# A hybrid encoder layer: the gate product placed eight expert blocks earlier, and its empty tiles lent to the expert loads

## The chip, the cores and the metric

The kernel runs on one core of one Trainium2 chip. The metric is device time in microseconds of that core, the median of several runs of one program. The engines are called as in the profile: PE (TensorE, matrix products), PEld (its weight loads), DVE (VectorE), ACT (ScalarE), POOL (GpSimd) and SP (SyncE, which here only issues transfers).

## The reference

One encoder layer on 512 tokens of width 1024. Attention comes first and is not touched. What matters is the part behind it:

```
q = xb @ w_q                                   # keys of 8 heads
v1, i1 = top_k(q1 @ sub_keys[0].T, 16)         # 16 of 128 first halves
v2, i2 = top_k(q2 @ sub_keys[1].T, 16)         # 16 of 128 second halves
cv, ci = top_k(v1[:, None] + v2[None, :], 16)  # 16 of 256 pairs -> expert e1*128 + e2
g   = softmax(cv)
act = g * gelu(xb . u_table[idx])
ffn = sum(act * v_table[idx])                  # 16384 experts, 128 per token
gate = sigmoid(h @ ple_gate_w + ple_gate_b)
h = layer_norm(alpha * h + ffn + gate * (p @ ple_w))
```

## The kernel before

The 512 tokens are four chunks of 128. Chunk 0 gets its expert rows by gathers from memory. For the other three chunks the whole expert table is multiplied: U block `i` (128 experts, 512 KB) times the tokens gives 128 x 256 values for chunks 2 and 3, and GELU of them is kept or written to memory (`ge_dram`). A matrix G (token by expert, the softmax weights) is built from products of one-hot tiles (`oh`, `ow_hi`, `ow_lo`) and written to memory (`g_dram`). Chunk 1 takes its first-layer values by gathered rows (128 of them, index tile `s_ix`), which land in six tiles (`whi`, `wlo`, `row`, two of each).

The change lies in the middle stage, from 414 to 909 us, which does all of this at once. Its order is written by hand in a manual schedule, in which every engine runs what it is given in the order of the program:

- DVE's own order is: routing of chunk 2 (`route`, the top-16 searches), building G of chunk 2 (`build_g`, 16 steps, each with a one-hot tile, two weighted tiles and a group of 16 products on PE), routing of chunk 3, building G of chunk 3, routing of chunk 0, building G of chunk 1. Row gathers of POOL and their dot products on DVE (L970) are put between these steps.
- PE gets, between these steps, `run_pe(amount)` worth of other work from one generator, `gate_and_leads`: 104 U blocks (`lead_block`, L1042, eight products over the tile `whole`), and the gate product in 16 sections of 12 products each (`mm<-g_hi,...`, L124 to L126). A section takes one weight tile (`g_raw`, 256 KB, L1063), cut by ACT into `g_hi` (L1070) and by DVE into `g_lo` (L1071). There is one `g_hi` and one `g_lo`, and three `g_raw`. Two U blocks stand behind each section (`STRIDE = 2`), and a third behind the eighth and the sixteenth, the two *gate ends*, where four 256 KB tiles `pl` are loaded (`gate_end`, L1079) and added by DVE with the bias tile `gb`.
- The first `FIRST` U blocks stand ahead of the gate. Fifteen blocks of the table were loaded long before into tiles that were empty then (`early`, `ge_ring`, `g_hi`, `base`); the order of blocks takes two of these and one fresh one in turn, until they are used up.
- SP issues the loads. A fresh U block goes to one of three tiles `raw` (`load_u`, L1015); `lead_block` issues loads until three are held, so that SP waits at each for PE to finish the block three before.
- Behind the gate, `own_h` splits `whole` again into the tiles `hTh`, with a copy on ACT (L1109) and a subtraction on POOL (L1113), in two halves, as tasks put between the blocks: the first half six blocks behind the gate's last task, the second two blocks later. POOL's row gathers stand before, between and behind them in its queue.

The tasks are taken one at a time, at every second product of a U block:

```
while sum(x[1] for x in held_u.values()) < 3 and to_load:
    load_u()
...
    if k % 2 and tasks:
        tasks.pop(0)()
    yield PRODUCT_U
```

Of the kernel before, what the change touches and what calls it, by code (L numbers as in the profile page):

```python
# [9 lines left out]
F32 = mybir.dt.float32  # L10
# [26 lines left out]
WIDE = 40  # L37
LEAD = 104
SPILL = 72
FIRST = 30  # L40
STRIDE = 2
PACE = 1.07
AHEAD = 14.0
# [35 lines left out]
def tile_encoder_layer(ctx: ExitStack, tc: tile.TileContext, A: dict, out: bass.AP):  # L79
    nc = tc.nc  # L80
# [104 lines left out]
    def ps_tile(name, bufs=2):  # L185
        return ps6.tile([128, 512], F32, name=name, bufs=bufs)
# [88 lines left out]
    with tc.tile_pool(name="ln0", bufs=1, reuse_waits="tile") as ln0:  # L275
# [5 lines left out]
        for c in range(4):  # L281
            layer_norm(h[c], eg, eb)
            transpose_to(hTh, hTl, h[c], c)
            if c == 0:
                for kk in range(4):
                    raw = wst.tile([128, 2, 512], F32, name="raw", bufs=3)
# [315 lines left out]
    for kk in range(4):  # L602
        w = stream(A["w_o"][kk * 256:(kk + 1) * 256, 0:512].rearrange("(k p) n -> p k n", p=128), [2, 512])
        for k2 in range(2):
            k = 2 * kk + k2
# [94 lines left out]
    rw = pR.enter_context(tc.tile_pool(name="rw", bufs=1, reuse_waits="tile"))  # L700
    h_s = rw.tile([128, D], F32, name="h_s")
    gb = rw.tile([128, D], F32, name="gb")
# [137 lines left out]
    for g in range(16):  # L840
# [7 lines left out]
        raw = wst.tile([128, 8, 128], F32, name="raw", bufs=3)  # L848
# [150 lines left out]
    gating = True  # L999
    held_u = {}  # L1000
# [7 lines left out]
    to_load = [i for i in lead_ids if i >= EARLY]  # L1008
    first_load = to_load[0]

    def load_u(name="raw"):
        if to_load:
            i = to_load.pop(0)
            raw_t = wst.tile([128, 8, 128], F32, name=name, bufs=3 if name == "raw" else 2)
            ins = nc.sync.dma_start(raw_t, A["uT"][i])  # L1015
            if i == first_load:
                tc.keep_in_program_order(ins)
            held_u[i] = ([raw_t[:, k] for k in range(8)], name == "raw")

    def leave_u(i, ps):  # L1020
        if i % 2 == 0:
            ge_t[i] = (ge_kept if SPILL <= i < KEPT else ge_free).pop(0)
        nc.scalar.activation(ge_t[i - i % 2][:, i % 2], ps[:, :N_U], AF.Gelu)  # L1023
        if i < SPILL and i % 2:
            x = ge_t.pop(i - 1)
            nc.scalar.dma_start(ge_dram[i // 2], x.rearrange("p b t -> p (b t)"))
            ge_free.append(x)
# [3 lines left out]
    def lead_block():  # L1031


        while sum(x[1] for x in held_u.values()) < 3 and to_load:
            load_u()
        if not lead_ids:
            return
        i = lead_ids.pop(0)
        raw = early_u[i] if i < EARLY else held_u.pop(i)[0]
        ps = psH.tile([128, 512], F32, name="hp") if gating else ps_tile("mm", 4)  # L1040
        for k in range(8):
            nc.tensor.matmul(ps[:, :N_U], raw[k], whole[:, k, :], start=(k == 0), stop=(k == 7))  # L1042
            if k == 3 and last:
                leave_u(*last.pop())
# [3 lines that stand above are left out]
        last.append((i, ps))  # L1048
# [11 lines left out]
    def gate_raw(j):  # L1060
        raw = rw.tile([128, 512], F32, name="g_raw", bufs=3)
        k = j % 8
        nc.sync.dma_start(raw, A["gate_w"][k * 128:(k + 1) * 128, j // 8 * 512:(j // 8 + 1) * 512])  # L1063
        return raw

    def gate_cut(raw):

        hi = rw.tile([128, 512], F32R, name="g_hi")
        lo = rw.tile([128, 512], F32R, name="g_lo")
        return (hi, lo), [lambda: nc.scalar.copy(hi, raw),  # L1070
                          on_vector(0.6, lambda: nc.vector.tensor_tensor(lo, raw, r32(hi), op=OP.subtract))]  # L1071
# [49 lines left out]
    def gate_and_leads():  # L1121
        nonlocal gating
        graw = [gate_raw(0), gate_raw(1)]
        for n in range(FIRST):
            if n == FIRST - 2:
                w, cut = gate_cut(graw.pop(0))
                tasks.extend([cut[0], nothing, cut[1]])
            yield from lead_block()
        for j in range(16):
            if j % 8 == 0:  # L1130
                while tasks:
                    tasks.pop(0)()
                gps = [ps_tile("mm", 4) for _ in range(4)]
            k = j % 8
            for c in range(4):
                cs = slice(c * 128, (c + 1) * 128)
                mm3(gps[c], (hTh[:, k, cs], hTl[:, k, cs]), w, k == 0, k == 7)
                yield PRODUCT_G
            if j + 1 < 16:
                w, cut = gate_cut(graw.pop(0))  # L1140
                if j + 2 < 16:
                    graw.append(gate_raw(j + 2))
                tasks[0:0] = [cut[0], nothing, cut[1]]
            if k == 7:
                gate_end(gps, slice(j // 8 * 512, j // 8 * 512 + 512))
                yield from lead_block()
            for _ in range(STRIDE):
                yield from lead_block()
# [32 lines left out]
    with tc.manual_schedule(engines={nc.vector.engine, nc.scalar.engine, nc.tensor.engine, nc.sync.engine,  # L1181
                                     nc.gpsimd.engine}):
        for _ in range(3):
            load_u()
# [63 lines left out]
    def load_v(n):  # L1248
        raw = wst.tile([128, D], F32, name="raw", bufs=3) if in_wst(n) else pV.tile([128, D], F32, name="v_raw", bufs=3)
        nc.sync.dma_start(raw, v_rows[order[n] * 128:(order[n] + 1) * 128, :])  # L1250
        return raw
# [55 lines left out]
    with tc.manual_schedule(engines={nc.vector.engine, nc.scalar.engine, nc.tensor.engine, nc.sync.engine,  # L1307
                                     nc.gpsimd.engine}):
        gating = True
        for name in ("whi", "whi", "wlo", "wlo"):  # L1310
            load_u(name)
        some = [fetch_u(0, BESIDE + k) for k in range(SOME)]
        for lo, hi in ((128 // GT, NTG), (0, 128 // GT)):
            load_g(0, lo, hi, nc.gpsimd)
        blocks_ahead(2)
        v_next = [load_v(n) for n in range(2)]
        for u in range(SOME):
            gather_u(0, BESIDE + u, some[u])
        blocks_ahead(2)
        v_next.append(load_v(2))  # L1320
        v_cut = {}
        for n in range(2):
            v_cut[n] = cut_v(n)
            blocks_ahead(1)
        for k in range(BESIDE + SOME, PRE):
            gather_u(0, k)
        for _ in pe_work:
            pass
# [7 lines left out]
    with tc.manual_schedule(engines={nc.vector.engine, nc.sync.engine}):  # L1336
# [3 lines left out]
        for n, i in enumerate(order):  # L1340
            if g_tiles and n == g_tiles[0][0]:
                n0, _, views, j = g_tiles.pop(0)
                gt = views[j]
            raw = v_next[n] if n < 3 else load_v(n)
# [149 lines left out]
```

## Time and profile before

| what | value |
|---|---|
| median of 3 runs | 1522.99 us (1522.4 to 1523.95) |
| profiled execution, its own time | 1525.05 us |
| its span, first to last instruction | 1523.2 us |
| mean granted TensorE clock | 0.990 |
| PE / DVE / ACT / POOL busy | 95% / 83% / 36% / 41% |
| bytes moved by DMA | 456 MB, mean 299 GB/s |

A row of a timeline reads: start in us, duration in us, engine, line, operation, the tile written and the tiles read, how many in a row; in brackets the idle time before it and who ended it. Matmuls are pipelined: their durations overlap, so that the pace of PE is read from the starts of successive rows. A line of windows gives a stretch, then the busy time of each engine with its count of instructions, the mean granted TensorE clock, the busy share of the DMA engines and the GB/s. One product of an fp32 U block stands in the trace as two PE instructions, so a U block is 16 of them. In the middle stage 414:507 is the routing of chunk 2, 507:591 building its G, 591:660 and 660:755 the same for chunk 3, 755:796 the routing of chunk 0, 796:878 building G of chunk 1, 878:909 the blocks left over.

### The profile page before, as it was taken

How to read it: one execution, taken by the hardware profiler on the slowest of the kernel's cores; microseconds unless marked ns; L12 is line 12 of the kernel's file. 1: busy time of each engine (PE TensorE's matmuls, PEld its weight loads, DVE VectorE, ACT ScalarE, POOL GpSimd, SP SyncE). 2: the span in 40 equal slices, each digit the busy share in tenths (PEclk: the TensorE clock that was granted, in tenths of full speed). 3: DMA queues.
4: the chain of work that ended last, by engine and by line, in shares of the span. 5: the costliest groups of instructions: out<-in, count | busy, mean ns of one | idle time of the engine just before them, and what ended most of it. 6: DMA issues, size and time to landing. Idle time of an engine off the chain costs nothing.

```text
span 1523.2 us, 21811 instructions
## 1 busy us (share of the span) xinstructions
PE 1451.8 (95%) x7715; PEld 1221.4 (80%) x7715; DVE 1267.5 (83%) x2638; ACT 544.4 (36%) x893; POOL 627.7 (41%) x537
## 2 busy tenths in 40 slices
PE   6999999999999999898989989999999999999996
PEld 4788777788888888687877868898788888888875
DVE  7376795668999999899779938988789999989998
ACT  3265685333311232222322323444333333333333
POOL 1013110043355644253235345655545555556560
PEclk9999999999999999899999999999999999999999
DMA  7233241194389999899879999999999999999992
GB/s 238 66 115 92 86 125 43 49 300 147 105 291 322 394 416 413 301 396 398 314 258 409 412 388 392 391 392 335 341 389 396 402 398 398 402 396 400 394 362 113
DMA packets 188414, 456.15 MB, mean 299 GB/s; under 512 B 16400, under 2 KB 80272, under 8 KB 185232
## 3 DMA queue, kind: packets, MB, share of 16 engines
q1 hardware_dynamic: 121264, 211.45, 38.8%
q0 software_dynamic: 58400, 208.69, 36.3%
q10 hardware_dynamic: 8640, 34.61, 5.6%
q8 instruction: 61, 1.00, 0.3%
q14 instruction: 49, 0.40, 0.1%
HBM read 413.01 MB, written 38.80 MB: 297 GB/s over the span
## 4 chain that ended last, share of the span: by engine, by line
PE 42%; DVE 20%; issue 15%; DMA 14%; POOL 6%; ACT 2%; SPq 1%; POOLq 0%; DVEq 0%; ACTq 0%
DMA raw<-in_v_rows_dram 7%; PE acc L126 5%; PE acc L124 5%; PE acc L125 5%; PE pj L124 3%; PE pj L125 3%; PE pj L126 3%; DMA raw<-in_uT_dram 3%; DVE base L1277 3%; PE mm L1042 3%; POOL row L968 2%; PE mm L124 2%; PE mm L126 2%; POOL wlo L968 2%; PE mm L125 2%
## 5 line engine op out<-in xcount | busy, mean ns | idle before, releaser
L1275 POOL DMA_INDIRECT gat<-in_v_rows_dram,i_sel x128 | 192.8, 1506 | 140.8 <-DVE base L1277 119.5
L1042 PE MATMUL hp<-whole,raw 128*128 128x256 f32 x816 | 193.4, 393 | 21.1 <-DMA raw<-in_uT_dram 21.1
L1260 POOL DMA_INDIRECT gat<-in_u_rows_dram,i_sel x97 | 149.4, 1541 | 121.8 <-DVE gat L1266 93.6
L1042 PEld LDWEIGHTS hp<-whole,raw 128*128 128x128 f32 x816 | 158.9, 197 | 45.6 <-issue 13.2
L126 PE MATMUL acc<-v_hi,a_lo 128*128 128x512 f32 x456 | 178.4, 392 | 2.6 <-DVE a_lo L110 2.5
L124 PE MATMUL acc<-v_hi,a_hi 128*128 128x512 f32 x456 | 178.3, 391 | 1.5 <-ACT v_hi L109 1.1
L125 PE MATMUL acc<-v_lo,a_hi 128*128 128x512 f32 x456 | 177.8, 390 | 0.8 <-DVE v_lo L110 0.8
L109 ACT CAST whi<-raw 128x1024 fp32r<-128x1024 f32 (+4 forms) x103 | 102.7, 997 | 198.7 <-DMA raw<-in_v_rows_dram 101.4
L1277 DVE SCALAR_TENSOR_TENSOR base<-gat,hdot,base 128x1024 f32<-128x1024 f32 x128 | 165.0, 1289 | 1.8
L110 DVE TENSOR_TENSOR wlo<-raw,whi 128x1024 fp32r<-128x1024 f32 (+4 forms) x103 | 118.6, 1152 | 42.7 <-ACT whi L109 41.8
L109 ACT CAST v_hi<-v_raw 128x1024 fp32r<-128x1024 f32 x76 | 79.9, 1052 | 144.7 <-DMA v_raw<-in_v_rows_dram 66.0
L1042 PE MATMUL mm<-whole,raw 128*128 128x256 f32 x560 | 126.7, 382 | 4.4 <-DMA raw<-in_uT_dram 4.4
L126 PE MATMUL acc<-whi,a_lo 128*128 128x512 f32 x312 | 121.6, 390 | 0.3 <-DVE a_lo L110 0.3
L125 PE MATMUL acc<-wlo,a_hi 128*128 128x512 f32 x312 | 121.5, 390 | 0.2 <-DVE wlo L110 0.2
L110 DVE TENSOR_TENSOR v_lo<-v_raw,v_hi 128x1024 fp32r<-128x1024 f32 x76 | 92.6, 1218 | 34.4 <-ACT v_hi L109 34.1
L124 PE MATMUL acc<-whi,a_hi 128*128 128x512 f32 x312 | 120.9, 389 | 0.0
L1266 DVE SCALAR_TENSOR_TENSOR gat<-gat,h 128x1024 f32<-128x1024 f32 x97 | 115.0, 1219 | 6.7 <-DMA gat<-in_u_rows_dram,i_sel 6.7
L1042 PEld LDWEIGHTS mm<-whole,raw 128*128 128x128 f32 x560 | 104.4, 190 | 18.8 <-DMA raw<-in_uT_dram 3.8
L126 PEld LDWEIGHTS acc<-v_hi,a_lo 128*128 128x128 f32 x456 | 85.6, 188 | 23.6 <-DVE a_lo L110 6.2
L124 PEld LDWEIGHTS acc<-v_hi,a_hi 128*128 128x128 f32 x456 | 85.6, 188 | 20.3 <-ACT a_hi L109 1.7
L125 PEld LDWEIGHTS acc<-v_lo,a_hi 128*128 128x128 f32 x456 | 85.7, 188 | 18.1 <-DVE v_lo L110 1.1
L1023 ACT ACTIVATE ge_ring<-hp 128x256 f32<-128x256 f32 x85 | 32.4, 381 | 146.0 <-PE hp L1042 123.9
(395 smaller groups left out, 3382.7 us busy)
## 6 DMA issues: line engine op xcount, KB each, us to landing
raw<-in_uT_dram SPq DMA_DIRECT2D x110, 512.0 KB
v_raw<-in_v_rows_dram SPq DMA_DIRECT2D x78, 512.0 KB
raw<-in_v_rows_dram SPq DMA_DIRECT2D x50, 512.0 KB
g_dram<-g_st ACTq DMA_DIRECT2D x24, 1024.0 KB
ge_dram<-ge_ring ACTq DMA_DIRECT2D x36, 256.0 KB
g_wide<-g_dram SPq DMA_DIRECT2D x9, 1024.0 KB
raw<-in_w_in_dram SPq DMA_DIRECT2D x17, 512.0 KB
raw<-in_w_q_dram SPq DMA_DIRECT2D x16, 512.0 KB
```

The source lines that it names most:

```text
L109: nc.scalar.copy(hi, src)
L110: nc.vector.tensor_tensor(lo, src, r32(hi), op=OP.subtract)
L124: nc.tensor.matmul(ps, a[0], b[0], start=start, stop=False)
L125: nc.tensor.matmul(ps, a[0], b[1], start=False, stop=False)
L126: nc.tensor.matmul(ps, a[1], b[0], start=False, stop=stop)
L968: nc.gpsimd.indirect_dma_start(out=u[:np], out_offset=None, in_=u_rows, in_offset=bass.IndirectOffsetOnAxis(ap=ix[:np, k:k + 1], axis=0))
L1023: nc.scalar.activation(ge_t[i - i % 2][:, i % 2], ps[:, :N_U], AF.Gelu)
L1042: nc.tensor.matmul(ps[:, :N_U], raw[k], whole[:, k, :], start=(k == 0), stop=(k == 7))
L1260: nc.gpsimd.indirect_dma_start(out=u[:], out_offset=None, in_=u_rows, in_offset=bass.IndirectOffsetOnAxis(ap=i_sel[:, c, k:k + 1], axis=0))
L1266: nc.vector.scalar_tensor_tensor(u, u, 1.0, h[c], op0=OP.mult, op1=OP.mult, accum_out=hdot[:, c, k:k + 1])
L1275: nc.gpsimd.indirect_dma_start(out=u[:], out_offset=None, in_=v_rows, in_offset=bass.IndirectOffsetOnAxis(ap=i_sel[:, c, k:k + 1], axis=0))
L1277: nc.vector.scalar_tensor_tensor(base[c], u, hdot[:, c, k:k + 1], base[c], op0=OP.mult, op1=OP.add)
```

## The change

`FIRST` becomes 22, so that the gate's first section stands behind 22 U blocks. Behind the gate (`gating` is false) U loads go in turn to the three `raw` tiles and to three places that the gate has left empty: `gb` whole, `g_hi` with `g_lo` as halves, two of the `g_raw` as halves. Six loads are held instead of three, while more than ten are left to load.

```
-FIRST = 30
+FIRST = 22
...
+    turn = [0]
+    def gate_place(j, i):
+        if j == 0:
+            x = rw.tile([128, 8, 128], F32, name="gb")
+            nc.sync.dma_start(x, A["uT"][i])
+            return [x[:, k] for k in range(8)]
+        names = ("g_hi", "g_lo") if j == 1 else ("g_raw", "g_raw")
+        ks = []
+        for half, n in enumerate(names):
+            x = rw.tile([128, 4, 128], F32, name=n, bufs=3 if j == 2 else 1)
+            nc.sync.dma_start(x, A["uT"][i][:, 4 * half:4 * half + 4])
+            ks += [x[:, k] for k in range(4)]
+        return ks
...
     def load_u(name="raw"):
         if to_load:
             i = to_load.pop(0)
+            if not gating and name == "raw" and len(to_load) > 10:
+                turn[0] += 1
+                if turn[0] % 6 >= 3:
+                    held_u[i] = (gate_place(turn[0] % 6 - 3, i), True)
+                    return
...
-        while sum(x[1] for x in held_u.values()) < 3 and to_load:
+        while sum(x[1] for x in held_u.values()) < (3 if gating or len(to_load) <= 10 else 6) and to_load:
             load_u()
```

The first place is PE's order where the gate begins. `tr<-ident` are the transposes that open the building of G of chunk 2. Before:

```order
L1042 MATMUL hp<-whole,early_4332 128x256 x8
L1042 MATMUL hp<-whole,early_4398 128x256 x8
L1042 MATMUL hp<-whole,raw 128x256 x8
L1042 MATMUL hp<-whole,base_3253 128x256 x8
L1042 MATMUL hp<-whole,raw 128x256 x34
L895 MATMUL tr<-ident,e_4945 128x128
```

and now:

```order
L1063 MATMUL hp<-whole,early_4332 128x256 x8
L1063 MATMUL hp<-whole,early_4398 128x256 x8
L1063 MATMUL hp<-whole,raw 128x256 x8
L1063 MATMUL hp<-whole,base_3253 128x256 x8
L124 MATMUL mm<-g_hi,hTh 128x512
L125 MATMUL mm<-g_lo,hTh 128x512
L126 MATMUL mm<-g_hi,hTl 128x512
```

The gate's first section stands right behind the last block that was loaded early, and two sections stand ahead of the transposes. Counted on in the same list, the first gate end moves from the routing of chunk 3 to a place behind the 12th of the 16 product groups of chunk 2, and the second from behind the 9th product group of chunk 3 to between its 1st and 2nd. From the 12th product group of chunk 3 on, PE's list has the same blocks at the same places as before.

The second place is SP's order at the second gate end. Before:

```order
L1063 DMA g_raw<-in_gate_w_dram 128x512
L1015 DMA raw<-in_uT_dram 128x1024 x4
L1079 DMA pl<-ple_dram 128x512 x4
L1015 DMA raw<-in_uT_dram 128x1024 x36
L1015 DMA whi<-in_uT_dram 128x1024
```

and now:

```order
L1084 DMA g_raw<-in_gate_w_dram 128x512
L1036 DMA raw<-in_uT_dram 128x1024 x4
L1100 DMA pl<-ple_dram 128x512 x4
L1036 DMA raw<-in_uT_dram 128x1024 x5
L1017 DMA gb<-in_uT_dram 128x1024
L1023 DMA g_hi<-in_uT_dram 128x512
L1023 DMA g_lo<-in_uT_dram 128x512
L1023 DMA g_raw<-in_uT_dram 128x512 x2
```

Behind the four `pl` loads five blocks still go to `raw` tiles; then three of six go to the gate's places, two of these as halves. The first gate end has the same rows in SP's order as before, with three tiles.

The third place is POOL's order at `own_h` (the rows `hTh`), with buffer numbers since the gathers read alike. Before:

```order
L968 DMA row_7256<-in_u_rows_dram,s_ix_3325 128x1024
L968 DMA whi_7275<-in_u_rows_dram,s_ix_3325 128x1024
L1113 TENSOR_TENSOR hTh_6979<-whole_3261,hTh_6979 128x1024
L968 DMA wlo_7302<-in_u_rows_dram,s_ix_3325 128x1024
L968 DMA row_7330<-in_u_rows_dram,s_ix_3325 128x1024
L1113 TENSOR_TENSOR hTh_6979<-whole_3261,hTh_6979 128x1024
L968 DMA whi_7348<-in_u_rows_dram,s_ix_3325 128x1024
```

and now:

```order
L968 DMA whi_6893<-in_u_rows_dram,s_ix_3325 128x1024
L968 DMA wlo_6917<-in_u_rows_dram,s_ix_3325 128x1024
L968 DMA row_6943<-in_u_rows_dram,s_ix_3325 128x1024
L1134 TENSOR_TENSOR hTh_6649<-whole_3261,hTh_6649 128x1024
L968 DMA whi_6966<-in_u_rows_dram,s_ix_3325 128x1024
L968 DMA wlo_7000<-in_u_rows_dram,s_ix_3325 128x1024
L968 DMA row_7034<-in_u_rows_dram,s_ix_3325 128x1024
L1134 TENSOR_TENSOR hTh_6649<-whole_3261,hTh_6649 128x1024
```

Of the 128 row gathers by `s_ix`, 121 stood ahead of the first subtraction and 123 ahead of the second; now 108 and 111. On ACT the first copy stood behind the output of the 16th and last product group of chunk 3; now it stands behind the 7th, and the second behind the 9th. The row of the first gather behind the subtraction is used by DVE behind `ow_lo` of the 10th step of chunk 3; before, in the routing of chunk 0.

## The prediction

> **What bounds the kernel now.** I read the head of the page first, then the windows of the middle stage, which the change touches, then PE's timeline there, reading only rows with an idle time.
>
> ```profile
> span 1523.2 us, 21811 instructions
> PE 1451.8 (95%) x7715; PEld 1221.4 (80%) x7715; DVE 1267.5 (83%) x2638; ACT 544.4 (36%) x893; POOL 627.7 (41%) x537
> DMA  7233241194389999899879999999999999999992
> ```
>
> PE is the busiest engine, but the DMA engines are full too in most of the slices behind the first third.
>
> ```profile
> core 0: us, PE busy (x) PEld busy (x) DVE busy (x) ACT busy (x) POOL busy (x), PEclk, DMA share, GB/s
> 414.00:507.00 93.00, 91.86 (x429) 80.53 (x428) 90.23 (x318) 18.11 (x35) 49.30 (x39) 1.00 0.86 298
> 507.00:591.00 84.00, 81.85 (x560) 70.56 (x559) 78.11 (x125) 26.40 (x54) 40.38 (x31) 1.00 1.03 415
> 591.00:660.00 69.00, 61.98 (x272) 52.88 (x272) 60.10 (x156) 13.40 (x27) 28.89 (x23) 0.93 0.90 343
> 660.00:755.00 95.00, 89.55 (x585) 77.38 (x584) 84.42 (x139) 28.12 (x60) 32.21 (x27) 0.96 0.96 372
> 755.00:796.00 41.00, 37.44 (x174) 32.43 (x172) 31.14 (x106) 9.64 (x18) 13.72 (x10) 1.00 0.74 269
> 796.00:878.00 82.00, 76.33 (x534) 66.35 (x535) 73.37 (x112) 23.49 (x51) 39.63 (x33) 1.00 1.01 404
> 878.00:909.00 31.00, 23.50 (x98) 19.63 (x96) 9.85 (x14) 7.12 (x12) 10.97 (x12) 0.89 1.02 383
> 909.00:1480.00 571.00, 566.43 (x2753) 476.88 (x2753) 510.77 (x572) 205.81 (x232) 328.76 (x212) 1.00 1.02 387
> ```
>
> The first seven rows are the middle stage. PE is busy 462.5 of 495 us there (the sum of the seven), so 32.5 us are its idle time. The granted clock falls in three (0.93, 0.96, 0.89). In the first, fourth and fifth stretches the DMA engines have room (298, 372, 269 GB/s); 415 GB/s is what they reach when full. The last row is the loop behind the stage: PE is idle in 4.6 of 571 us, so what the stage saves or loses goes through to the end.
>
> ```profile
> 506.29 1.10 PE L1042 MATMUL hp<-whole,raw 128*128 128x256 f32 x4 [1.14 <-DMA raw<-in_uT_dram]
> 622.92 6.48 PE L1042 MATMUL hp<-whole,raw 128*128 128x256 f32 x16 [7.02 <-DMA raw<-in_uT_dram]
> 629.04 0.58 PE L124 MATMUL mm<-g_hi,hTh 128*128 128x512 f32 x1
> 632.00 7.07 PE L1042 MATMUL hp<-whole,raw 128*128 128x256 f32 x32
> 638.72 0.58 PE L124 MATMUL mm<-g_hi,hTh 128*128 128x512 f32 x1
> 722.03 6.42 PE L1042 MATMUL hp<-whole,raw 128*128 128x256 f32 x16 [5.45 <-DMA raw<-in_uT_dram]
> 728.28 2.75 PE L1042 MATMUL mm<-whole,raw 128*128 128x256 f32 x12
> 770.09 23.55 PE L1042 MATMUL mm<-whole,raw 128*128 128x256 f32 x108 [1.42 <-DMA raw<-in_uT_dram]
> 796.45 0.33 PE L895 MATMUL tr<-ident,gws 128*128 128x128 f32 x1 [2.60 <-DVE w_top L994]
> 831.33 2.86 PE L1042 MATMUL mm<-whole,raw 128*128 128x256 f32 x12 [1.11 <-DMA raw<-in_uT_dram]
> 850.10 0.70 PE L1042 MATMUL mm<-whole,raw 128*128 128x256 f32 x2 [1.84 <-DMA raw<-in_uT_dram]
> 892.57 6.49 PE L1042 MATMUL hp<-whole,raw 128*128 128x256 f32 x16 [6.44 <-DMA raw<-in_uT_dram]
> ```
>
> PE waits for U blocks, and three of the waits are long. Two U blocks take 638.72 - 632.00 = 6.72 us, one 3.36. The block behind the first long wait took 629.04 - 622.92 = 6.12, the one behind the second 728.28 - 722.03 = 6.25: 2.76 and 2.89 us more, at a fallen clock:
>
> ```profile
> 616.00:623.00 7.00, 0.08 (x1) 0.12 (x1) 6.90 (x13) 2.06 (x5) 1.88 (x2) 0.67 1.04 411
> 623.00:635.00 12.00, 12.00 (x42) 9.91 (x43) 5.03 (x8) 0.90 (x2) 0.94 (x1) 0.77 0.62 228
> ```
>
> PE idled, the granted clock went from 2.4 to 1.2 GHz within the first row and came back in the second; the DMA engines, full at 411 GB/s during the wait, then ran half empty because DVE and the gathers had stalled behind PE. So the first long wait costs 7.02 + 2.76 = 9.78 us and the second 5.45 + 2.89 = 8.34. Both stand behind the gate ends, as SP's own timeline shows:
>
> ```profile
> 603.74 1.84 SPq L1079 DMA_DIRECT2D pl<-ple_dram  x4
> 606.88 9.38 SPq L1015 DMA_DIRECT2D raw<-in_uT_dram  x3
> 701.00 1.94 SPq L1079 DMA_DIRECT2D pl<-ple_dram  x4
> 705.03 28.18 SPq L1015 DMA_DIRECT2D raw<-in_uT_dram  x5
> ```
>
> Four `pl` loads (1 MB) go ahead of the U loads, and three blocks stand in a row behind that section. The load issued at 606.88 lets PE go on at 622.92, 16.0 us later; the one at 705.03 at 722.03, 17.0 us. With three tiles a load has the time of two blocks (6.7 us) and what stands between them.
>
> **The first gate end** moves into the building of G of chunk 2, still with three tiles. Two product groups and part of another section now stand in the run of blocks, so PE needs the late block a little later; but the DMA engines are as full there (415 GB/s, the 507 row) and ACT writes G at the same time. Ends: all 9.78 us go; or, with G's writes as a third drawer beside U and the gathers, the load takes half as long again, 24 us: 8 us more. I take 0, the wait as it is, since the row is nearest to it.
>
> **The second gate end** moves to the first product groups of chunk 3, before its first G tile is written. Fewer bytes compete there, and the order puts two product groups between its blocks. Ends: all 8.34 us go, or none. I take 1.5 us left: -6.8. The gate's products themselves are only moved.
>
> **Six tiles.** From there on a load has the time of five blocks, 16.8 us at PE's pace, about what the slowest loads above took. The waits at 770.09, 831.33 and 850.10 (4.37 us) and the one at 506.29 (1.14, where gate sections now thin out the loads) should go; the last, 6.44 at 892.57, stays, because the last ten loads have three tiles again. Ends: -5.5 and 0. I take -1.4 at 770, -2.95 and -1.1. Three more blocks held are 1.5 MB more to move in chunk 3, 3.8 us at 415 GB/s, against free room of (415 - 372) x 95 us = 4.1 MB there. Ends: 0 and +3.8; I take +1.0. The ten or so extra SP instructions of the half blocks are hidden by SP's waits for PE.
>
> **`own_h`** moves from the routing of chunk 0 into the middle of chunk 3.
>
> ```profile
> 754.39 1.08 ACT L927 ACTIVATE g_st<-tr 128x512 f32<-128x512 f32 x2 [2.54 <-PE tr L916]
> 755.88 1.04 ACT L1109 CAST hTh<-whole 128x1024 fp32r<-128x1024 f32 x1 [0.40 <-ACT g_st L927]
> 757.00 2.35 POOL L1113 TENSOR_TENSOR hTh<-whole,hTh 128x1024 fp32r<-128x1024 f32 x1 [16.41 <-ACT hTh L1109]
> 759.50 0.95 POOL L968 DMA_INDIRECT wlo<-in_u_rows_dram,s_ix  x1
> 765.02 1.23 DVE L970 SCALAR_TENSOR_TENSOR wlo<-wlo,h_s 128x1024 f32<-128x1024 f32 x1 [7.15 <-DMA wlo<-in_u_rows_dram,s_ix]
> ```
>
> POOL runs six gathers ahead, so it waits 16.41 us for ACT's copy; the gather behind it lands 5.5 us after its issue, and DVE has waited 7.15 us. DVE is then late for `w_top`, for which PE waits 2.60 us at 796.45. At the old place this goes: -2.6 (ends -2.6 and 0). At the new place I lay the same steps beside DVE's of before:
>
> ```profile
> 696.02 0.23 PE L916 MATMUL tr<-ow_hi,oh 128*128 128x128 f16 x1
> 707.38 0.68 DVE L949 TENSOR_TENSOR ow_lo<-oh,w_lo 128x1024 f16<-128x1024 f16 x1
> 708.59 1.21 DVE L970 SCALAR_TENSOR_TENSOR whi<-whi,h_s 128x1024 f32<-128x1024 f32 x1
> ```
>
> The copy stands behind the 7th group of chunk 3 (696.02). Allowing 1 us for the group, then 1.08, 1.04, 2.35 and 5.5, the row lands at 707.0. DVE wants it behind the 10th `ow_lo`, about 708.6. It is just in time. Ends: 0, or the old wait twice, for POOL's two subtractions are three gathers apart: 2 x (7.15 + 2.8 of slow clock) = 19.9. I take +1.5.
>
> **The sum:** 0 - 6.8 - 1.4 - 2.95 - 1.1 + 1.0 - 2.6 + 1.5 = -12.35 us. The profiled execution took 1525.05, its span 1523.2 and 1.85 around it; that makes 1512.7. The median shown is 2.06 lower, so the forecast is 1522.99 - 12.35 = 1510.6. About 3 us, 0.2%, is what a measurement can tell from no change.
>
> **Rivals.** *Full engines:* The stage may be bound by bytes, so that six loads in the air only take from the gathers what they give to U. For it speak 415 and 404 GB/s in the building of G; against it 343, 372 and 269 beside them, the half-empty 12 us behind the wait at 616, and PE's list, which is not short of work. Then only the 2.6 at `w_top` goes and 1.0 and 1.5 come: about 1522.9, no change. The Trainium skill, DMA: Bandwidth & Descriptors, section Issuing engines are not separate DMA queues, says that transfers of SP, ACT and POOL all run on the same 16 engines and interleave: by that rule a longer queue adds no bandwidth, and the forecast would be this rival's. The trace agrees for the full stretches, and does not for the others.
>
> *Starved gathers (the other side):* if the copy of `own_h` runs over 1.6 us later than I laid it, or a gather lands that much later than 5.5 us among full engines, DVE waits at both subtractions, in the middle of chunk 3, where PE needs DVE's tiles for every group, and not in a long run of blocks as before (108 instructions in the row 770.09). The price is 19.9 instead of 1.5: 1510.6 + 18.4 = 1529.0. The chain that decides it leaves 1.6 us, which is little; for the forecast speaks that DVE will itself be later, by the second gate end's additions, now ahead of that place.
>
> *Both gate ends free:* the product groups and sections between the blocks are enough at the first end as well: 1510.6 - 9.8 = 1500.8.
>
> *The gate waits for its weights:* DVE cuts `g_lo` in its own order and is as busy as PE in the new place (90.2 of 93 us), so PE could wait for it ahead of sections one and two. A cut stands behind a DVE instruction or two at most, 1.21 us for the longest kind in the rows above, so 2.4 us for two sections: 1513.0, inside the range; at the gate's old place no PE row shows such a wait.
>
> **How the numbers follow.** The forecast with the wait for weights, 0.54 (1506 to 1516); both ends free, 0.12; full engines, 0.18; starved gathers, 0.16. The range 1499 to 1526 takes in the first three; it leaves out the starved gathers and a few hundredths below. Under 1520 lie the first two and a little of the third: faster 0.69; the rest of the third and the edge of the others: same 0.14; slower 0.17.
>
> **What would show it.** The block behind which the gate now begins is the one that lay in `base`:
>
> ```profile
> L1042 PE MATMUL hp<-whole,base x16: 379/379/380, 487.7 to 491.0; 128*128 128x256 f32 x16
> L124 PE MATMUL mm<-g_hi,hTh x64: 387/397/586, 522.2 to 707.9; 128*128 128x512 f32 x64
> ```
>
> So the first gate product should start near 491 us instead of 522.2. A wait of 5 to 9 us for a U block, and a fallen clock, stands behind the 12th product group of chunk 2, and none over 2 us behind the second gate end. PE's waits for `raw` between 750 and 860 are gone and that for `w_top` too; the last of 6 us is still there. POOL waits at both `hTh` subtractions, DVE under 2 us for the rows behind them. The prediction is wrong if DVE waits there for 5 us or more, if the first gate end's wait grows past 10 us, or if waits for row gathers on DVE take up what PE no longer waits for.

## The result, and the profile after

The changed kernel took a median of 1516.87 us (1512.38 to 1518.11, 6 runs), beside 1524.10 us for the kernel before in the same measurement (1522.40 to 1526.57): a ratio of 0.9949, 95% interval [0.9934, 0.9964]. Two more measurements of the same kernel, told below, gave 0.9968 and 0.9959. So 4 to 7 us are gone, where the forecast took 12.35 away. The profiled execution took 1517.09 us, its span 1515.3.

Three profiles of the changed kernel have spans of 1515.3, 1518.0 and 1517.1 us, so that a difference of less than 3 us between two single spans says nothing by itself.

The head of the page, and the windows of the middle stage at the same landmarks as before (the borders lie up to 6 us elsewhere, because the landmarks do):

```profile
span 1515.3 us, 21825 instructions
PE 1450.1 (96%) x7715; PEld 1221.1 (81%) x7715; DVE 1269.2 (84%) x2638; ACT 543.5 (36%) x893; POOL 624.4 (41%) x537
```

```profile
414.00:508.00 94.00, 94.00 (x440) 82.24 (x438) 91.23 (x321) 19.40 (x37) 49.41 (x39) 1.00 0.86 292
508.00:592.00 84.00, 74.57 (x504) 64.40 (x502) 81.33 (x123) 24.87 (x52) 36.22 (x31) 0.97 1.03 414
592.00:660.00 68.00, 67.89 (x320) 58.31 (x321) 56.02 (x155) 13.95 (x27) 27.86 (x23) 0.96 0.91 343
660.00:756.00 96.00, 86.96 (x570) 75.24 (x569) 83.02 (x125) 28.48 (x59) 44.05 (x34) 0.98 1.00 390
756.00:793.00 37.00, 37.00 (x183) 32.66 (x181) 34.70 (x124) 8.50 (x17) 5.24 (x6) 1.00 0.80 299
793.00:875.00 82.00, 80.81 (x561) 70.89 (x560) 75.24 (x113) 25.11 (x54) 41.52 (x34) 1.00 1.01 405
875.00:903.00 28.00, 22.61 (x103) 19.26 (x101) 9.63 (x13) 6.31 (x10) 9.82 (x10) 0.88 1.02 382
```

The routing of chunk 2 and the routing of chunk 0 (first and fifth row) now have no idle PE, and chunk 3 moves 390 GB/s instead of 372. The long wait has gone from chunk 3's routing into chunk 2 (second row: PE busy 74.57 of 84). PE's timeline, with the landmarks and the rows that waited longest:

```profile
491.11 0.58 PE L124 MATMUL mm<-g_hi,hTh 128*128 128x512 f32 x1
592.11 3.33 PE L1063 MATMUL hp<-whole,raw 128*128 128x256 f32 x7 [9.35 <-DMA raw<-in_uT_dram]
682.96 2.28 PE L1063 MATMUL hp<-whole,raw 128*128 128x256 f32 x5 [2.98 <-DMA raw<-in_uT_dram]
727.39 0.23 PE L916 MATMUL tr<-ow_hi,oh 128*128 128x128 f16 x1 [1.26 <-DVE ow_hi L949]
729.14 0.22 PE L916 MATMUL tr<-ow_lo,oh 128*128 128x128 f16 x1 [1.51 <-DVE ow_lo L949]
734.29 0.22 PE L916 MATMUL tr<-ow_lo,oh 128*128 128x128 f16 x1 [0.16 <-DVE ow_lo L949]
748.65 0.22 PE L916 MATMUL tr<-ow_lo,oh 128*128 128x128 f16 x1 [1.00 <-DVE ow_lo L949]
755.78 0.22 PE L916 MATMUL tr<-ow_lo,oh 128*128 128x128 f16 x1 [2.13 <-DVE ow_lo L949]
794.01 0.27 PE L895 MATMUL tr<-ident,gws 128*128 128x128 f32 x1
882.79 2.50 PE L1063 MATMUL hp<-whole,raw 128*128 128x256 f32 x5 [5.09 <-DMA raw<-in_uT_dram]
899.06 0.47 PE L124 MATMUL hp<-hTh,whi 128*128 128x256 f32 x1
```

The gate begins at 491.11, where the block in `base` ended. The waits for U blocks at 506, 770, 831 and 850 us are gone, and so is the one for `w_top`: `gws` starts at 794.01 without a wait. Three things are not gone: the first gate end's wait (9.35), a smaller one at the second (2.98), and the last (5.09). Five waits for DVE are new, 6.06 us in sum, all in chunk 3 behind `own_h` (6.00 and 2.46 us in the two other profiles).

Landmarks of PE say where the time went. The last column adds up the terms of the prediction that fall into each stretch:

| from, to | before | after | difference | second profile | third profile | forecast |
|---|---|---|---|---|---|---|
| start, transposes of chunk 2 | 507.23 | 508.00 | +0.77 | +0.62 | +1.46 | -1.1 |
| to the transposes of chunk 3 | 152.34 | 152.31 | -0.03 | -0.22 | -1.09 | 0 |
| to the transposes of chunk 1 (`e1s`) | 133.90 | 133.48 | -0.42 | -0.46 | -1.53 | -5.7 |
| to the transpose of `gws` | 2.98 | 0.22 | -2.76 | -2.76 | -2.76 | -2.6 |
| to the loop's first product | 112.62 | 105.05 | -7.57 | -3.47 | -7.10 | -2.95 |
| to the end of the span | 614.1 | 616.2 | +2.1 | +1.1 | +4.9 | 0 |

PE stands at the transposes of chunk 1 no earlier than before (0.06 and 1.16 us earlier in the other two profiles): up to 793 us, which is where the whole gate moved, it gained next to nothing net. The gain lies behind that point.

### The profile page after: what moved, and what is told of

Its sections match the earlier page's. It is cut to its first block, busy times and chain, and to the rows that moved or that the text cites. A ratio compares the mean times of both kernels' runs of the same rounds, so it can differ in the third digit from the quotient of the medians.

```text
span 1515.3 us, 21825 instructions
## 1 busy us (share of the span) xinstructions
PE 1450.1 (96%) x7715; PEld 1221.1 (81%) x7715; DVE 1269.2 (84%) x2638; ACT 543.5 (36%) x893; POOL 624.4 (41%) x537
## 4 chain that ended last, share of the span: by engine, by line
PE 52%; DVE 20%; DMA 14%; issue 8%; POOL 3%; ACT 2%; SPq 1%; DVEq 0%; POOLq 0%; ACTq 0%
PE acc L126 6%; PE acc L124 6%; PE acc L125 6%; PE hp L1063 6%; DMA raw<-in_uT_dram 4%; PE pj L124 3%; DMA raw<-in_v_rows_dram 3%; PE pj L126 3%; PE pj L125 3%; PE mm L124 3%; DMA v_raw<-in_v_rows_dram 3%; PE mm L126 3%; PE mm L125 2%; DVE base L1298 2%; DMA wlo<-in_u_rows_dram,s_ix 2%
## 5 line engine op out<-in xcount | busy, mean ns | idle before, releaser
L1063 PE MATMUL hp<-whole,raw 128*128 128x256 f32 x688 | 162.7, 392 | 17.4 <-DMA raw<-in_uT_dram 17.4
L1063 PEld LDWEIGHTS hp<-whole,raw 128*128 128x128 f32 x688 | 133.6, 196 | 37.6 <-issue 12.8
L1063 PE MATMUL mm<-whole,raw 128*128 128x256 f32 x400 | 91.2, 381 | 0.0
L1063 PEld LDWEIGHTS mm<-whole,raw 128*128 128x128 f32 x400 | 74.7, 190 | 9.4
L968 POOL DMA_INDIRECT whi<-in_u_rows_dram,s_ix x43 | 52.7, 1225 | 64.6 <-DVE whi L970 38.4
```

The lines of the kernel that those rows point to most:

```text
L968: nc.gpsimd.indirect_dma_start(out=u[:np], out_offset=None, in_=u_rows, in_offset=bass.IndirectOffsetOnAxis(ap=ix[:np, k:k + 1], axis=0))
```

## The experiments

Each of the three batches was timed beside runs of the kernel before on the same chip. Diffs are against the changed kernel.

**Three tiles throughout.** Only the gate's new place is kept:

```
-            if not gating and name == "raw" and len(to_load) > 10:
+            if False and not gating and name == "raw" and len(to_load) > 10:
...
-        while sum(x[1] for x in held_u.values()) < (3 if gating or len(to_load) <= 10 else 6) and to_load:
+        while sum(x[1] for x in held_u.values()) < 3 and to_load:
```

> Only the gate's place is changed (22 blocks ahead of it), U loads keep three tiles throughout. My theory: the gain of the change lies behind the building of G of chunk 3 and needs both halves; the early gate alone moves the split of own_h out of the routing of chunk 0, so the 2.6 us wait for w_top goes, and the long wait at the second gate end goes; the waits for U blocks between 755 and 860 us (4.4 us) stay. About 3 to 5 us faster than the kernel before, ratio 0.997 to 0.998. Rival (full engines: six tiles give nothing): the early gate alone gives the whole 7 us, ratio 0.995.

Measured: 1.0004 [0.9990, 1.0017]. The gate's place by itself is worth nothing, against what I expected. PE's timeline:

```profile
684.63 2.90 PE L1063 MATMUL hp<-whole,raw 128*128 128x256 f32 x6 [3.41 <-DMA raw<-in_uT_dram]
738.11 0.22 PE L916 MATMUL tr<-ow_lo,oh 128*128 128x128 f16 x1 [3.70 <-DVE ow_lo L949]
832.46 2.86 PE L1063 MATMUL mm<-whole,raw 128*128 128x256 f32 x12 [2.17 <-DMA raw<-in_uT_dram]
```

The second gate end is as short as in the changed kernel, and `own_h` costs its DVE waits (3.70 here, 1.52 at 729.41), but the waits for U blocks at 832 and 850 (1.31 there) are back. So it is the six tiles, not the gate's place, that remove those. The gate's place did remove the wait for `w_top` and shorten the second gate end, but PE stands at the transposes of chunk 1 at 798.07 us, 4.6 later than before; which rows make this up was not taken apart.

**Six tiles, gate at its old place.**

```
-FIRST = 22
+FIRST = 30
```

> Only the six tiles are added, the gate stays behind 30 blocks. My theory: the long waits of about 7 and 5.5 us behind the two gate ends stay, since both still have three tiles; the U waits at 770, 831 and 850 us go; the split of own_h stays in the routing of chunk 0 with its 7 us wait on DVE and 2.6 us on PE. 2 to 4 us faster than the kernel before, ratio 0.997 to 0.999. Rival (full engines): no gain, ratio 1.000, since waits for row gathers on DVE grow by what the U waits lose.

Measured: 0.9977 [0.9966, 0.9987]. Both gate ends are as before (waits of 8.01 and 4.61 us), no wait for a U block between 756 and 879 exceeds 1 us, and the one for `w_top` stays:

```profile
798.15 0.47 PE L895 MATMUL tr<-ident,gws 128*128 128x128 f32 x1 [4.62 <-DVE w_top L994]
```

Alone, the halves are worth nothing and 3.1 us (1519.46 beside 1522.58); together 4 to 7.

**`own_h` back in the routing of chunk 0**, with the gate early and six tiles:

```
-        tasks.extend([nothing] * 24)
+        tasks.extend([nothing] * 56)
```

> The changed kernel with the split of own_h put 8 blocks later (32 more empty tasks), back into the routing of chunk 0. My theory: PE's six waits for DVE in the second half of chunk 3 (6.1 us in all) come from POOL's 10 us wait at the split and the gathers late behind it; they shrink to under 2 us, and chunk 3 ends 4 to 5 us earlier; DVE then waits some 7 us in the routing of chunk 0, and PE some 2.6 us for w_top again, so that 1 to 3 us are left: ratio to the kernel before 0.993 to 0.994, against 0.995 of the changed kernel. Rival (full engines): the six tiles take the gathers' share of the DMA engines, the waits of PE for DVE in chunk 3 stay at 4 us or more, and the whole is no faster than the changed kernel or slower by the wait for w_top, 0.995 to 0.997.

Measured: 0.9991 [0.9980, 1.0002], slower than the changed kernel and than either expectation. The DVE waits in chunk 3 are gone (one of 3.28 us for ACT stands there now), and PE is at the transposes of chunk 1 at 789.47 instead of 793.79 us. But there the old wait returns, doubled, because DVE waits for its gathered row. DVE first, then PE:

```profile
764.95 1.22 DVE L970 SCALAR_TENSOR_TENSOR wlo<-wlo,h_s 128x1024 f32<-128x1024 f32 x1 [8.29 <-DMA wlo<-in_u_rows_dram,s_ix]
```

```profile
794.96 0.48 PE L895 MATMUL tr<-ident,gws 128*128 128x128 f32 x1 [5.11 <-DVE w_top L994]
```

So `own_h` has a price at either place: the early one cost PE 6.06, 6.00 and 2.46 us of waits in three profiles, the late one 5.11 in its one. By the loop's first product PE stands where it does in the changed kernel (899.68, there 898.05 to 902.78); the rest takes 619.5 us, against 615.2 to 619.0, and why is open.

**`own_h`'s two subtractions on DVE instead of POOL.**

```
-            nc.gpsimd.tensor_tensor(hi_lo[:, 1, ks], whole[:, ks], r32(hi_lo[:, 0, ks]), op=OP.subtract)
+            nc.vector.tensor_tensor(hi_lo[:, 1, ks], whole[:, ks], r32(hi_lo[:, 0, ks]), op=OP.subtract)
...
-            tasks.extend([lambda x=x: hi(x), nothing, nothing, lambda x=x: lo(x)] + [nothing] * 4)
+            tasks.extend([lambda x=x: hi(x), nothing, nothing, on_vector(1.2, lambda x=x: lo(x))] + [nothing] * 4)
```

> The changed kernel with the two subtractions of own_h on DVE instead of POOL. My theory: PE's 6.1 us of waits for DVE in the second half of chunk 3 come from POOL's 10 us wait at the first subtraction, which holds back the row gathers behind it; with the subtractions on DVE, POOL does not wait, these waits fall to about 2 us, DVE has 2.4 us more to do, and the whole is 1 to 4 us faster than the changed kernel (0.992 to 0.994 of the kernel before). Rival (full engines): the gathers are late because the six tiles take their share of the DMA engines; PE's waits for DVE stay at 4 us or more and the 2.4 us come on top, so 0 to 3 us slower than the changed kernel (0.995 to 0.997).

Measured: 0.9981 [0.9969, 0.9993], where the changed kernel beside it gave 0.9968 [0.9955, 0.9982]: no better, and slower than either expectation. The first steps are as expected. POOL no longer stands in front of its gathers, and of PE's waits in chunk 3 those for DVE are gone; one for ACT is there instead. PE starts chunk 1's first group 2 us earlier. Then the last wait is 10.97 us, where the profile of the changed kernel beside it has 6.75:

```profile
754.02 0.22 PE L916 MATMUL tr<-ow_hi,oh 128*128 128x128 f16 x1 [2.61 <-ACT g_st L927]
887.25 3.36 PE L1063 MATMUL hp<-whole,raw 128*128 128x256 f32 x7 [10.97 <-DMA raw<-in_uT_dram]
```

**The `pl` loads one at a time**, at the fourth to the seventh section of each half of the gate, instead of four together at its end:

```
+    def load_pl(c, hs):
+        pl[c] = rg.tile([128, 512], F32, name="pl", bufs=4)
+        nc.sync.dma_start(pl[c], ple_dram[c, :, hs])
...
-        for c in range(4):
-            load(c)
...
+            if 3 <= k <= 6:
+                load_pl(k - 3, slice(j // 8 * 512, j // 8 * 512 + 512))
```

> The changed kernel with the four pl loads of each gate end issued one at a time in the four sections ahead of it. My theory: the 9.35 us wait for a U block behind the first gate end is due to the 1 MB of pl loads that stand ahead of three U loads in SP's queue; spread, the wait falls to under 4 us and the clock does not fall for as long: 5 to 9 us faster than the changed kernel, ratio to the kernel before 0.989 to 0.992. Rival (full engines): at 415 GB/s the U blocks wait for their share wherever pl stands; the waits are only spread over several blocks, and the ratio stays at 0.994 to 0.996.

Measured: 0.9928 [0.9909, 0.9948], and again in the second batch:

> The spread pl loads once more beside the changed kernel on one chip. My theory: 2.5 to 6 us faster than the changed kernel (ratio to the kernel before 0.991 to 0.993). Rival (full engines): within 2 us of it.

0.9902 [0.9886, 0.9918], 1508.93 us, against 0.9968 [0.9955, 0.9982] and 1519.50 us for the changed kernel beside it, a larger gain than expected:

> The changed kernel itself once more, on the same chip as the other runs of this call, so that they can be compared with it: 0.994 to 0.996 of the kernel before by every theory.

This is the fastest version of all that ran. In place of the 9.35 and 2.98 us stand short waits, the first of them for an addition of DVE (the second profile of this kernel):

```profile
590.19 0.50 PE L124 MATMUL mm<-g_hi,hTh 128*128 128x512 f32 x1 [1.32 <-DVE base L1111]
876.67 3.78 PE L1063 MATMUL hp<-whole,raw 128*128 128x256 f32 x8 [5.38 <-DMA raw<-in_uT_dram]
```

The clock holds too. The stretch of the first gate end, in the changed kernel and then with spread loads:

```profile
585.00:592.00 7.00, 0.00 (x0) 0.00 (x0) 6.37 (x10) 1.07 (x2) 0.72 (x1) 0.69 1.04 413
592.00:604.00 12.00, 11.89 (x49) 9.83 (x50) 3.22 (x6) 1.99 (x4) 0.94 (x1) 0.76 0.50 182
```

```profile
585.00:592.00 7.00, 5.31 (x25) 3.88 (x22) 6.90 (x11) 1.16 (x2) 1.76 (x2) 1.00 1.03 412
592.00:604.00 12.00, 11.26 (x74) 9.19 (x73) 11.86 (x30) 3.96 (x9) 3.57 (x3) 1.00 0.82 298
```

The DMA engines are as full in the first stretch (413 and 412 GB/s); what differs is how soon a U load lands. Of the loads issued from 566 to 594 us, with the number of loads, their size and the median us from issue to landing, in the changed kernel and then with spread loads:

```profile
raw<-in_uT_dram SPq DMA_DIRECT2D x4, 512.0 KB, 16.1
```

```profile
raw<-in_uT_dram SPq DMA_DIRECT2D x5, 512.0 KB, 7.4
```

Only the place of the `pl` loads differs between the two kernels. So it was the megabyte of `pl` in front of the U load, not full engines as such, that made the wait. Two more pairs of kernels below differ in this alone, and gain 7.2 and 8.2 us by it.

**Both together**, spread loads and subtractions on DVE:

> Both: pl loads spread over four sections and the subtractions of own_h on DVE. If both costs are separate, as in my theory, their gains add: about 0.990 of the kernel before. If what is freed in one place is only waited for in the next (rival, full engines), it is no faster than the spread loads alone, 0.993.

Measured: 0.9928 [0.9915, 0.9942], not better than spread loads alone (0.9902). The gains do not add. The waits for DVE right behind `own_h` are gone, but others stand in chunk 3, 3.33 us in sum (with spread loads alone 3.11 and 4.45 us in all), and PE comes to the transposes of chunk 1 at 785.11 us, no earlier than with spread loads alone (781.94 and 782.83). So nothing was freed there that the last wait, 11.46 us here, could take back.

**Six tiles until two are left**, to see what the last wait is. In the changed kernel, then with spread loads, `10` becomes `2` in both places; a third run repeats the changed kernel beside them:

```
-            if not gating and name == "raw" and len(to_load) > 10:
+            if not gating and name == "raw" and len(to_load) > 2:
...
-        while sum(x[1] for x in held_u.values()) < (3 if gating or len(to_load) <= 10 else 6) and to_load:
+        while sum(x[1] for x in held_u.values()) < (3 if gating or len(to_load) <= 2 else 6) and to_load:
```

> The changed kernel, with six U blocks in the air until two are left to load instead of ten. Open is why PE's last wait for a U block (6.44 us at 892 us before, 5.1 and 6.8 in two profiles of the changed kernel) stays, and grew to 11 where own_h runs on DVE. Theory: with three tiles the last blocks are asked for too late; then the last wait falls under 2 us, the loop's first product starts 4 to 6 us earlier and the time is 0.992 to 0.994 of before. Rival: from 793 us on the DMA engines are full (1.01 of their time in 793 to 875 and 1.02 in 875 to 903), so the wait is for bytes; then asking earlier only moves it: PE's waits for raw behind 850 us, and for the loop's first tiles, stay at 5 us or more in sum, and the time is that of the changed kernel, 0.995 to 0.997.

> The spread pl loads (0.990 and 0.993 of before), with six U blocks in the air until two are left. PE comes to the last blocks 8 to 10 us earlier here than in the changed kernel. Theory of the late request: the last wait of 4.9 to 5.4 us goes under 2 and the time falls to 0.986 to 0.990 of before. Rival of full engines: 0.990 to 0.993 as without it, with waits of 5 us or more somewhere between 850 and 900 us.

> The changed kernel again, beside the two others on the same chip: 0.995 to 0.997 of before by every theory. Its profile tells how much the last wait (5.1 and 6.8 us so far) differs between executions of one kernel.

Measured: 0.9982 [0.9971, 0.9993] and 0.9927 [0.9912, 0.9942], against 0.9959 [0.9945, 0.9972] for the changed kernel. The last wait is gone, the loop begins earlier (894.07 instead of 898.05 in the profile beside it), and PE waits there instead, first for its own loads, as the rival said. PE's rows of the changed kernel with six tiles until two are left:

```profile
894.07 0.38 PE L124 MATMUL hp<-hTh,whi 128*128 128x256 f32 x1 [1.36 <-ACT whi L109]
897.39 0.58 PE L126 MATMUL hp<-hTh,wlo 128*128 128x256 f32 x1 [2.82 <-DVE wlo L110]
906.98 0.58 PE L126 MATMUL hp<-hTh,wlo 128*128 128x256 f32 x1 [5.14 <-DVE wlo L110]
912.80 0.39 PE L124 MATMUL hp<-hTh,whi 128*128 128x256 f32 x1 [1.06 <-ACT ge_ring L1044]
```

That is 10.38 us, instead of 4.81 (0.49 and 4.32, the last waits in the third profile of the changed kernel) and 1.45 in its loop's first products. But 0.9982 is slower than the rival expected too, and its condition, full engines, does not hold in this run. The stretch from 870 to 880 us and SP's first U loads of the loop, in the third profile of the changed kernel and then in this run:

```profile
870.00:880.00 10.00, 7.29 (x39) 5.82 (x36) 2.65 (x6) 2.23 (x5) 3.13 (x3) 0.99 1.01 375
874.20 28.45 SPq L117 DMA_DIRECT2D raw<-in_uT_dram  x5
```

```profile
870.00:880.00 10.00, 8.94 (x54) 7.82 (x52) 3.78 (x7) 2.23 (x5) 3.37 (x4) 1.00 0.75 272
878.93 28.35 SPq L117 DMA_DIRECT2D raw<-in_uT_dram  x5
```

What SP waited for in this run from 866 to 882 us (us in total, times, the longest):

```profile
SPq L1036 <- DVE whi L970: 13.9, 2, 7.2
```

With the blocks before them asked for early, SP stood at the last blocks' `whi` tiles until DVE had used the gathered rows in them, and the loop's loads stood behind that in its queue: they went out 4.7 us later, and the engines had a hole. The hole is about 1 MB, (375 - 272) x 10 us, or some 2.7 us at the loop's 388 GB/s; the medians differ by 3.0. So this run does not tell whether the last wait is for bytes or for a late request: the edit moved a wait and opened a gap.

**The bytes up to 793 us.** The windows of one stretch of fixed length, 414 to 793 us, and of the one behind it, to 903, for the changed kernel and for spread loads in its second profile:

```profile
414.00:793.00 379.00, 360.42 (x2010) 312.86 (x2009) 346.29 (x843) 95.19 (x192) 162.78 (x130) 0.98 0.93 354
793.00:903.00 110.00, 103.42 (x662) 90.15 (x660) 84.88 (x126) 31.42 (x64) 51.33 (x44) 0.97 1.02 399
```

```profile
414.00:793.00 379.00, 367.00 (x2046) 317.05 (x2045) 353.75 (x849) 97.12 (x197) 170.97 (x136) 0.99 0.95 364
793.00:903.00 110.00, 102.60 (x656) 89.71 (x655) 86.25 (x129) 32.66 (x63) 50.42 (x42) 0.94 1.01 392
```

Behind 793 the engines are full (1.02 and 1.01). The same row of every profile, with the span; the third column is (GB/s - 349) x 379 us, and the fourth is that at the loop's 388 GB/s:

| kernel | GB/s, 414 to 793 | MB against before | us at 388 GB/s | span against before, us |
|---|---|---|---|---|
| before | 349 | 0 | 0 | 0 |
| three tiles | 348 | -0.4 | +1.0 | 0.0 |
| six tiles, late gate | 354 | 1.9 | -4.9 | -1.4 |
| changed, three profiles | 354, 354, 355 | 1.9 to 2.3 | -4.9 to -5.9 | -7.9, -5.2, -6.1 |
| `own_h` later | 355 | 2.3 | -5.9 | -4.0 |
| six tiles until two are left | 355 | 2.3 | -5.9 | -3.1 |
| `own_h` on DVE | 357 | 3.0 | -7.8 | -7.1 |
| spread, six until two are left | 361 | 4.5 | -11.7 | -11.9 |
| spread, `own_h` on DVE | 363 | 5.3 | -13.7 | -11.8 |
| spread, two profiles | 364, 364 | 5.7 | -14.7 | -15.2, -14.5 |

The bytes moved by 793 us give the span within 3.5 us for kernels that differ in their waits all through the stage. Three kernels gained less than their bytes for a reason that PE's rows show: six tiles with the late gate, and `own_h` later, wait for `w_top` behind 793, with engines not quite full there (shares of 0.97 and 0.99 in 793 to 903); six tiles until two are left waits in the loop, behind its hole. This is a reading of one table, not an experiment on bytes: no run took bytes out behind 793 us with all else kept. Nor does the table say which is the cause, since a kernel whose PE is further on at 793 us has also asked for more of its loads.

## Why the forecast was right in sign and too large

The forecast was -12.35 us; the three measurements give -7.2, -4.4 and -5.6 us as differences of medians. By the landmarks the largest shortfall lies between the transposes of chunk 3 and of chunk 1: 0.4 to 1.5 us came there instead of 5.7, since the second gate end and `own_h` were sized too well. The start lost 1.7 to 2.6 us against the forecast and the part behind the loop's first product 1.1 to 4.9; between `gws` and the loop 0.5 to 4.6 us more came than forecast. By the prediction's own terms:

- **First gate end, 0: right in the sum, by luck.** Its wait grew from 7.02 to 9.35 and the slow clock behind it costs 12 x (1 - 0.76) = 2.9 us, 2.4 more than before together. Two waits for DVE that stood beside it before, and that the prediction did not name, went in return, 1.51 and 0.64:

```profile
584.13 0.22 PE L916 MATMUL tr<-ow_lo,oh 128*128 128x128 f16 x1 [1.51 <-DVE ow_lo L949]
589.94 0.22 PE L916 MATMUL tr<-ow_lo,oh 128*128 128x128 f16 x1 [0.64 <-DVE ow_lo L949]
```

  Both profiles need 152.3 us from the transposes of chunk 2 to those of chunk 3. The rule of the first gate end is what the prediction read from the old one: the U load behind the four `pl` lets PE go on 16 to 17 us after its issue. SP's rows show it again, 592.11 - 574.69 = 17.4:

```profile
567.75 2.04 SPq L1100 DMA_DIRECT2D pl<-ple_dram  x4
574.69 8.37 SPq L1036 DMA_DIRECT2D raw<-in_uT_dram  x3
```

- **Second gate end, -6.8: half of it came.** The wait is 2.98 and the slow stretch behind it (683 to 690 us, granted clock 0.76) costs 7 x (1 - 0.76) = 1.7: 4.7 of 8.34 are left, not 1.5, which makes -3.7. The product groups between the blocks did not cover a load that stands behind the `pl` loads with three tiles. That `pl` is the cause is shown by the spread loads, which take away both gate ends. The same wait is 3.03 and 3.40 us in the two other profiles.
- **U wait at 770, -1.4, and at 831 and 850, -2.95: right.** They are gone with six tiles and there with three. From the first to the last group of chunk 1 PE needs 69.1 us (800.96 to 870.05), where it needed 72.7 (804.53 to 877.21): -3.6.
- **U wait at 506, -1.1: the wait is gone, but nothing came of it.** The transposes of chunk 2 stand 0.77 us later. The two gate sections that now lie ahead of them take about 2 us more of PE than the block they replace; the prediction moved the gate's products without charging the landmark. It comes back in chunk 3.
- **Bytes of three more blocks, +1.0: no row shows such a cost.** Chunk 3 moved 390 instead of 372 GB/s, in room that was there; and in the table more bytes moved early go with a shorter span.
- **`w_top`, -2.6: right,** -2.76 by the landmarks.
- **`own_h` at its new place, +1.5: mis-sized, at least 2.5 to 3.3.** POOL's rows, then DVE's waits, in the first profile:

```profile
712.75 2.55 POOL L1134 TENSOR_TENSOR hTh<-whole,hTh 128x1024 fp32r<-128x1024 f32 x1 [10.05 <-ACT hTh L1130]
715.45 1.23 POOL L968 DMA_INDIRECT whi<-in_u_rows_dram,s_ix  x1
720.71 2.36 POOL L1134 TENSOR_TENSOR hTh<-whole,hTh 128x1024 fp32r<-128x1024 f32 x1
```

```profile
724.24 1.23 DVE L970 SCALAR_TENSOR_TENSOR whi<-whi,h_s 128x1024 f32<-128x1024 f32 x1 [3.76 <-DMA whi<-in_u_rows_dram,s_ix]
753.89 1.23 DVE L970 SCALAR_TENSOR_TENSOR wlo<-wlo,h_s 128x1024 f32<-128x1024 f32 x1 [2.07 <-DMA wlo<-in_u_rows_dram,s_ix]
```

  The row gathered at 715.45 was wanted at 720.48 and used at 724.24, at most 8.8 us after its issue, where I took 5.5: the engines are full here. The wait of 3.76 us for it is over the 2 us that the prediction had set as a sign, and stands in all three profiles (3.81 and 3.44 in the others); PE loses 2.5 to 3.3 us right behind it. The wait at 753.89, some 30 us later, is 1.84 in the second profile and missing in the third, and with it some 3 us of PE's waits; whether it belongs to `own_h` is open. The rival of starved gathers was this mechanism at a third of its price or less, since POOL waits at the first subtraction only (the second has no wait) and PE has blocks of its own between the groups. With the subtractions on DVE the waits right behind `own_h` are gone, in the changed kernel and with spread loads (3.11 and 3.36 us there), so POOL's wait makes these.

- **What the stage saves goes through: 1 to 5 us too much credited.** To the loop's first product PE gained 10.0, 6.3 and 11.0 us in the three profiles, and from there to the end it took 2.1, 1.1 and 4.9 us more than before. PE's own loop has no slack, and that is why I let the gain through; but the DMA engines are full there too (1.02). That loads which come no earlier are what is lost there is likely, and not shown by a run. The last wait (5.09, 6.75 and 4.32 us) the prediction had left standing; it is no part of this.

**The rivals.** *Full engines* is refuted for the stage up to 793 us: it forecast no gain but `w_top`, and six tiles alone gave 0.9977 with that wait still there; and spreading 2 MB of loads, without a byte less, brought the ratio from 0.9968 to 0.9902. For the part behind 793 it is open: the engines are full there in the changed kernel, but the run meant to decide it left a hole in them. The Trainium skill, DMA: Bandwidth & Descriptors, section Issuing engines are not separate DMA queues, says that transfers from all issuers share the same 16 engines and interleave; the trace agrees where the share is 1.02, and the 182 GB/s at half share behind the first gate end shows that it settles nothing where the engines run empty. *Gate waits for its weights*: no row of PE waits for `g_hi` or `g_lo` in the changed kernel. *Both gate ends free* (1500.8) needed the spread loads, and came to 1508.9 to 1511.2 there.

Why the two halves need each other is only partly settled. The early gate frees the six tiles some 40 us sooner, so that they can fill chunk 3's room; without them its place earns `w_top` and half the second gate end, and pays `own_h` and the waits for U blocks that stay. That the sums come out at nothing and at 4 to 7 us is consistent with the table of bytes; it was not taken apart further.

## What to carry to other kernels

Before crediting a removed wait, look at the DMA share of everything behind it: where the engines are full to the end, part of the gain can be lost again, here 1 to 5 us. Variants that had moved more bytes before the full stretch ended sooner; that it is the bytes is not shown. Look at what stands ahead of an urgent load in its own queue: four loads that nobody needed yet, issued in one go at each of two places, cost 7 to 11 us together in three pairs of kernels, and issuing them one by one cost 2.4 us of short waits. Three tiles too few cost 3.1 us beside the late gate and 5 to 8 beside the early one. A load asked for too early can do the same harm, when its tile is not free and the queue waits with it. A wait on a gather queue that was taken out of one place showed up in the next; price it with the gather's duration in that place, not in the old one, and look at more than one profile: PE's waits behind this one were 2.5 us in one profile and 6 in two others.

## What had not been expected of the hardware

The bytes moved between 414 and 793 us went with the end of the span to within 3.5 us over nine variants, although PE is busy in 96% of the span and the DMA engines move only 301 GB/s on the mean. POOL's subtraction of 128x1024 takes 2.36 and 2.55 us in the first profile of the changed kernel; the same on DVE takes 1.22 where it was put there:

```profile
716.84 1.22 DVE L1134 TENSOR_TENSOR hTh<-whole,hTh 128x1024 fp32r<-128x1024 f32 x1
```
